# A hybrid decoder trunk: the order of TensorE's work written out by hand, projections in steps of 12 matmuls with mixer pieces between them

## The chip, the cores and the metric

The kernel runs on one core of a Trainium2 chip. The core has TensorE (PE, matmuls and transposes into PSUM), VectorE (DVE), ScalarE (ACT) and GpSimd (POOL) for elementwise work, and SyncE (SP), which issues the DMAs. Each engine runs its instructions in the order in which they stand in its queue and waits on semaphores for what the others produce. The metric is the device time of one execution in microseconds (us).

## The reference

The reference does one inference step of a 2-layer trunk of width 1024: 2048 prompt tokens from zero states, and 8 sample tokens from stored states. Cut to what matters:

```python
def hybrid_layer(x, ...):                     # called for layer 0 and 1, prompt and sample
    hn = rms_norm(x, norm_w)
    proj = hn @ w_in                          # 1024 -> 13 pieces, 256 wide; m_xbc is 512, m_dt 4
    r_q, r_k, r_v, r_g, g_q, g_f, g_i, g_g, s_u, s_g, m_z, m_xbc, m_dt = split(proj)
    o_ret  = head_rms(retention(rotary(r_q), rotary(r_k), r_v)) * silu(r_g)      # a, RetNet
    o_hgrn = head_rms(recurrence(silu(g_q), k(g_f), g_i, log_f(g_f))) * silu(g_g) # h, HGRN2
    gy     = gelu(s5_scan(s_u) + s5_D * s_u)                                      # s, S5
    o_s5   = gy * sigmoid(gy @ s5_glu_w + s5_glu_b) * silu(s_g)
    xbc    = silu(causal_conv(m_xbc))                                             # m, Mamba-2
    o_m2   = rms((ssd(xbc, softplus(m_dt)) + m2_D * xm) * silu(m_z)) * m2_norm_w
    return x + concat(o_ret, o_hgrn, o_s5, o_m2) @ w_out, final_states
```

A final RMSNorm follows. The outputs are both token streams and the six final states of each kind.

## The kernel before

The prompt goes through in 8 blocks: 2 layers of 4 blocks of `TB` = 512 tokens. The 8 sample tokens ("decode") ride along in the first block of each layer, that is in blocks 0 and 4. A block has nine phases: four input projections A, H, S and M, the mixers a, h, s and m that work on their results, and the output projection O. n and N are the norm of the next block.

A projection works in fp32 through TensorE's rounded format: each weight tile `wr` arrives by DMA, ACT casts it to a high part `wh` (L606, L642), DVE subtracts to get the low part (L607, L643), and PE does three matmuls (low times high, high times low, high times high) for each weight tile and token tile. `gemm` handles 256 columns (L590 with tokens on the output's partitions, L622 with columns on them), `gemm_wide` 512 columns (L647). Both hold their result in PSUM banks `gb` and read them out when all 8 slices of the contraction are done. The mixers, the norm and the decode step use banks `mb`. The two pools hold at most `NGP` = 5 and `NMP` = 3 banks.

The mixer h is a recurrence in seven levels. Each level has a small set of matmuls (L1183, the last level L1198) on a zero-padded copy of the queries that ACT writes (`zb`, L1176), then DVE merges the result under a mask (L1191) and scales queries and keys (L1204, L1205), from which ACT makes the next level's copy. m uses such a copy too, and the two buffers are handed out in turn (`zbuf`). s runs through matmuls L1284, a scan on DVE, matmuls L1332, transposes L1339 with a gelu on ACT (L1340), matmuls L1345 and a gate on DVE (L1348 to L1352), which writes the operand `mx` of O. a and m write theirs through transposes in `mix_store` (L663). L849 and L886 belong to the decode step.

What sets the order: the phases are emitted as the string `ORDER` says, one after the other, where `^` means the block before. This order gives the instructions their priorities. A list scheduler, at build time, then orders every engine's instructions, PE's too, by those priorities and its own model of when operands are there. The lines:

```python
ORDER = 'A-n^s-H-a-^OMh-SNm'
ORDER_LAST = 'A^sSa^OsHhMm'
```

So PE's queue is fixed when the kernel starts, and a mixer's few matmuls stand wherever the scheduler had them ready. WPRI, SPRI, DPRI and EPRI are offsets of priority for weight loads, the set-up of S5, decode, and the read-out of banks.

## Time and profile before

| | |
|---|---|
| median of 3 runs | 2356.22 us (2350.71 to 2357.18) |
| span of the profiled execution | 2351.3 us |
| time around it | 4.9 us to the median of the runs |
| PE busy | 2186.8 us, 93% |
| DVE busy | 1690.8 us, 72% |
| ACT busy | 1007.4 us, 43% |
| POOL busy | 247.0 us, 11% |
| mean granted TensorE clock | 0.973 |

An engine's busy time is the union of its instructions' spans. What is left to the span is idle, and a wait is put down to the instruction on another engine that ended last before it. A group of rows joins all instructions of one line, operation and operands; its mean is longer than its spacing, since matmuls overlap in the pipeline. In the timeline a row is a run of equal instructions: start, length, and in brackets the idle time before it with its releaser.

### The profile page before, as it was taken

To read this page: it belongs to the slowest core of one execution; us is meant where nothing else is said; L and a number is where in the kernel's file an instruction comes from. 1 tells how busy PE (TensorE), PEld (TensorE's weight loads), DVE (VectorE), ACT (ScalarE), POOL (GpSimd) and SP (SyncE) were. 2 spreads that over 40 slices of the span, in tenths; PEclk is the share of its full clock that TensorE was granted. 3 is DMA by queue.
4 is the path that set the end of the run, shared out by engine and by line. 5 is a ranking of instruction groups with operands and counts; after the bars stand their busy time and mean duration, and the time that the engine had idled before them with its cause. 6 is when DMAs were issued, how large, how long until landed. Compare 5 with 4: busy or idle time off the path is not lost.

```text
span 2351.3 us, 41033 instructions
## 1 busy us (share of the span) xinstructions
PE 2186.8 (93%) x15047; PEld 1724.8 (73%) x15047; DVE 1690.8 (72%) x4625; ACT 1007.4 (43%) x1873; POOL 247.0 (11%) x212
## 2 busy tenths in 40 slices
PE   7997899999989999999899987999999999999897
PEld 6766676686767877788676775776877787777687
DVE  6778885578866687558856588855985568766686
ACT  5334545245442353424534245443454344443543
POOL 1020011001111011001110001100011001100100
PEclk9998899999999999999999998999999999999998
DMA  5334543433434644251333424526244352337222
GB/s 190 89 95 103 159 154 76 129 107 118 133 101 147 139 126 141 75 167 47 125 126 114 134 65 153 162 46 182 86 153 157 104 175 64 95 122 260 64 65 83
DMA packets 259226, 283.89 MB, mean 121 GB/s; under 512 B 88208, under 2 KB 184608, under 8 KB 259024
## 3 DMA queue, kind: packets, MB, share of 16 engines
q1 hardware_dynamic: 259024, 281.26, 39.8%
q8 instruction: 119, 1.95, 0.3%
q14 instruction: 83, 0.68, 0.1%
HBM read 245.00 MB, written 31.99 MB: 118 GB/s over the span
## 4 chain that ended last, share of the span: by engine, by line
PE 57%; DVE 20%; issue 6%; ACT 3%; DMA 2%; SPq 1%; POOL 1%; ACTq 0%; DVEq 0%; POOLq 0%
PE gb L647 25%; PE gb L622 10%; PE gb L590 5%; DVE big L1191 2%; PE mb L1332 1%; PE mb L1183 1%; DVE wh L643 1%; PE mb L569 1%; DMA big<-s5c 1%; DVE hHb L1240 1%; DVE half L1299 1%; PE gb L652 1%; PE mb L663 1%; SPq L940 1%; PE mb L1198 1%
## 5 line engine op out<-in xcount | busy, mean ns | idle before, releaser
L647 PE MATMUL gb<-wh,hn 128*128 128x512 f32 x2208 | 558.0, 402 | 4.9 <-DVE wh L643 4.3
L622 PE MATMUL gb<-hn,wh 128*128 128x512 f32 x1920 | 491.5, 403 | 0.1
L647 PEld LDWEIGHTS gb<-wh,hn 128*128 128x128 f32 x2208 | 408.1, 190 | 110.3 <-issue 13.5
L622 PEld LDWEIGHTS gb<-hn,wh 128*128 128x128 f32 x1920 | 348.9, 188 | 89.4 <-issue 8.8
L642 ACT CAST wh<-wr 128x512 fp32r<-128x512 f32 x296 | 182.7, 620 | 375.9 <-PE gb L647 184.5
L647 PE MATMUL gb<-wh,mx 128*128 128x512 f32 x1344 | 338.0, 402 | 0.0
L643 DVE TENSOR_TENSOR wh<-wr,wh 128x512 fp32r<-128x512 f32 x296 | 208.6, 712 | 170.5 <-ACT wh L642 169.6
L607 DVE TENSOR_TENSOR wh<-wr,wh 128x512 fp32r<-128x512 f32 (+1 forms) x248 | 176.9, 724 | 169.5 <-ACT wh L606 163.6
L647 PEld LDWEIGHTS gb<-wh,mx 128*128 128x128 f32 x1344 | 247.7, 189 | 63.5 <-issue 6.9
L606 ACT CAST wh<-wr 128x512 fp32r<-128x512 f32 (+1 forms) x248 | 151.6, 621 | 268.1 <-PE gb L647 103.8
L590 PE MATMUL gb<-wh,hn 128*128 128x256 f32 (+1 forms) x1728 | 233.3, 291 | 4.2 <-DVE hn L553 4.1
L590 PEld LDWEIGHTS gb<-wh,hn 128*128 128x128 f32 x1728 | 218.2, 194 | 13.3 <-DVE hn L553 5.9
L1445 POOL TENSOR_TENSOR half<-mats,m_lal 128x512 fp32r<-128x512 f32 x64 | 71.7, 1148 | 511.1 <-DVE m_lal L1423 301.6
L1183 PE MATMUL mb<-zb,big 128*64 128x64 f32 x1536 | 66.5, 242 | 38.8 <-ACT zb L1176 31.5
L1191 DVE COPY_PREDICATED big<-lvl,mb 64x256 f32<-64x256 int32 x192 | 93.0, 537 | 10.3 <-PE mb L1183 6.4
L1176 ACT COPY zb<-big 64x512 f32<-64x512 f32 x112 | 70.3, 628 | 64.0 <-DVE big L1204 54.2
L1183 PEld LDWEIGHTS mb<-zb,big 128*64 128x64 f32 x1536 | 56.6, 152 | 53.5 <-ACT zb L1176 38.2
L1166 POOL TENSOR_TENSOR big<-mats,h_dg 128x1024 f32<-128x1024 f32 x16 | 34.0, 2140 | 557.8 <-DVE h_dg L1163 438.5
L1367 DVE SCALAR_TENSOR_TENSOR big<-gb,vt,big 128x511 f32<-128x511 f32 (+2 forms) x96 | 66.9, 739 | 12.0 <-ACT big L1365 11.8
L671 ACT ACTIVATE half<-mb 128x512 f32<-128x512 f32 x32 | 19.1, 598 | 88.3 <-PE mb L1227 47.8
L1348 DVE TENSOR_TENSOR half<-half,big 128x512 f32<-128x512 f32 x16 | 10.9, 687 | 63.1 <-ACT half L1347 63.1
L1042 POOL TENSOR_TENSOR half<-half,half 128x256 f32<-128x256 f32 x32 | 27.2, 850 | 235.0 <-DVE half L1040 85.2
(493 smaller groups left out, 3240.7 us busy)
## 6 DMA issues: line engine op xcount, KB each, us to landing
wr<-in_w_in SPq DMA_DIRECT2D x416, 256.0 KB
wr<-in_w_out SPq DMA_DIRECT2D x128, 256.0 KB
big<-s5c SPq DMA_DIRECT2D x56, 512.0 KB
xn<-xmid SPq DMA_DIRECT2D x32, 512.0 KB
xn<-in_x_prompt SPq DMA_DIRECT2D x24, 512.0 KB
xmid<-half SPq DMA_DIRECT2D x44, 256.0 KB
half<-xmid SPq DMA_DIRECT2D x44, 256.0 KB
half<-in_x_prompt SPq DMA_DIRECT2D x32, 256.0 KB
```

Of the source, the lines that this page charges most:

```text
L590: T.matmul(out, lhs[2 * ks[ki] + k][:, a, tt * P : (tt + 1) * P], hls[ki][:, c, k, :n], start=(ki == 0 and k == 0 and pi == 0 and tt % per ...
L606: S.copy(hl[:, 0, :, :n], raw[:, :, :n])
L607: V.tensor_tensor(hl[:, 1, :, :n], raw[:, :, :n], hl[:, 0, :, :n].bitcast(F32), ALU.subtract)
L622: T.matmul(banks[i], hl[:, a, k, i * P : (i + 1) * P], lhs[2 * k2 + k][:, c, :], start=(ki == 0 and k == 0 and pi == 0), stop=(ki == 3 and ...
L642: S.copy(hl[:, 0, 0:512], raw[:, 0:512])
L643: V.tensor_tensor(hl[:, 1, 0:512], raw[:, 0:512], hl[:, 0, 0:512].bitcast(F32), ALU.subtract)
L647: T.matmul(banks[tt], lhs[kt][:, a, tt * P : (tt + 1) * P], hl[:, c, 0:512], start=(kt == 0 and pi == 0), stop=(kt == KT - 1 and pi == 2))
L1176: S.copy(qz[sl, r, :].rearrange("p (b h) -> p b h", h=h), q[sl].rearrange("p a (b two h) -> p (a b) two h", two=2, h=h)[:, :, 1, :])
L1183: T.matmul(ps[su, j * 64 : (j + 1) * 64], k[:, j // 4, (j % 4) * P + 64 * u : (j % 4) * P + 64 * u + 64], qz[:, :, j * 64 + 32 * u : j * 6 ...
L1191: V.copy_predicated(stv[p][su, :, nu * u : nu * u + nu, :], mv, ps[su, p * 256 : p * 256 + 256].rearrange("p (c b h) -> p c b h", c=8, h=h))
L1367: V.scalar_tensor_tensor(acc[:, 3 - i :], ps[:, : TB - 3 + i], w(i), acc[:, 3 - i :], ALU.mult, ALU.add)
L1445: E('m').tensor_tensor(mm.rearrange("p (h t) -> p h t", h=4), tri[:, None, :].to_broadcast([P, 4, P]), lal[:, i, tt, :][:, :, None].to_bro ...
```

## The change

PE leaves the scheduler: `tc.manual_schedule` with PE alone keeps PE's instructions in the order in which the program emits them. DVE, ACT, POOL and SP are still ordered by the scheduler. To emit PE's work in a useful order, projections and mixers become generators. A projection yields after each step of 12 matmuls of 512 columns (or 24 of 256 or 260). `run` calls `tick` after each step, and `tick` lets at most two ready mixer streams (lanes m, s, a, h) and one of decode, layer load and set-up (lanes d, e, f, p) emit one piece each. `yield n` in a mixer says how many ticks to wait until its next piece. The core of the diff:

```diff
-ORDER = 'A-n^s-H-a-^OMh-SNm'
-ORDER_LAST = 'A^sSa^OsHhMm'
-EPRI = 0
+EPRI = 100
-DW = 2
-NWR = 7
-NWH = 6
+DW = 4
+NWR = 6
+NWH = 5
-NBIG = 9
+NBIG = 10
-NGP = 5
-NMP = 3
+NGP = 4
+NMP = 4
...
-    zbs = [ctile([P, 2, TB], f"zb{i}") for i in range(NZ)]
+    zbH, zbM = ctile([P, 2, TB], "zbH"), ctile([P, 2, TB], "zbM")
...
     def gemm_wide(lhs, w, c0, evac, dec=None):
...
+        for kt in range(KT - 2):
+            load(kt)
+            for tt in range(4):
+                t_pass(kt, tt)
+            dec_pass(kt)
+            yield
+        load(KT - 2)
+        load(KT - 1)
         for tt in range(4):
+            t_pass(KT - 2, tt)
+            t_pass(KT - 1, tt)
             with tc.high_priority(offset=EPRI):
                 evac(tt, banks[tt])
+            if tt == 1:
+                yield
...
     def mix_H(L, B):
...
+            yield 2
+            pss = []
             if l < 6:
                 ps = mbank()
...
+    def tick():
+        clock[0] += 1
+        for names, most in (("msah", 2), ("defp", 1)):
+            for st in front(names)[:most]:
+                st.step()
+
+    def drain(*streams):
+        for _ in range(10000):
+            left = [st for st in streams if st is not None and not st.done]
+            if not left:
+                return
...
+            min(heads, key=lambda st: st.ready).step()
+
+    def run(gen, each=None):
+        for n, _ in enumerate(gen):
+            if each is not None:
+                each(n)
+            tick()
...
+    with tc.manual_schedule(engines={mybir.EngineType.PE}):
...
+        for i, B in enumerate(blocks):
+            run(ga if i == 0 else gemm_A(B.L, B))
+            run(gemm_H(B.L, B))
+            if B.prev is not None:
+                finish(B.prev, ("a", B), ("h", B), parts=(0, 1) if nxt is not None else (0,))
...
+                run(gemm_M(B.L, B))
+                begin("m", B)
...
+                run(gemm_S(B.L, B), lambda n: next(norm, 0) if n >= 3 else None)
...
+                begin("s", B)
...
+            else:
+                run(gemm_S(B.L, B))
+                begin("s", B)
+                run(gemm_M(B.L, B))
+                begin("m", B)
+                finish(B.prev, parts=(1,))
+                finish(B)
```

`finish` runs O of the block given, here with a and h of the next block as streams beside it; `front` gives the streams whose waiting time is over, and `begin` starts a stream. The last two slices of `gemm_wide` are done bank by bank, so each bank is read out while the next is still filled; `gemm` does the same in its last step. Further edits: the decode step's bank comes from the `mb` pool, RV stands before RQ in A except in the first block, a is split into scores, state, inter and mixed pieces that overlap over token tiles, s loads its tables in halves, and s waits for h (`B.hdone`). In the last block, whose O has no later projections to stand beside, `drain` emits what is left of a, h, s and m in one go.

The instructions are the same on PE (11825 matmuls and transposes), DVE and POOL. ACT has 92 table loads in the program where it had 72, and there are 40 more DMAs (1290, 1250 before). In PE's order the projections' matmuls stand in 532 uninterrupted runs before and in 307 after; those 512 wide in 442 and in 265, and of the 442, 251 were shorter than 6 matmuls, of the 265 none.

On PE, the recurrence of h in the third block (`zb` is the padded copy, `hn` the projections' operand):

```order
L590 MATMUL gb_8632<-wh_8692,hn_5910 128x256 x5
L1183 MATMUL mb_8318<-zb_114,big_6968 64x64 x16
L590 MATMUL gb_8632<-wh_8692,hn_5910 128x256
L590 MATMUL gb_8633<-wh_8692,hn_5910 128x256 x6
L590 MATMUL gb_8632<-wh_8721,hn_5923 128x256 x2
L1183 MATMUL mb_8348<-zb_113,big_6968 64x64 x8
L590 MATMUL gb_8632<-wh_8721,hn_5923 128x256 x4
L590 MATMUL gb_8633<-wh_8721,hn_5923 128x256
L1183 MATMUL mb_8348<-zb_113,big_6968 64x64 x8
```

And now, where the levels of h (L1293) stand beside the output projection (L687) of the block before, with a's pieces (L1173 to L1202) and the decay sums (L1163):

```order
L1293 MATMUL mb_10209<-zbH,big_9640 64x64 x16
L687 MATMUL gb_10029<-wh_10239,mx_9932 128x512 x3
L687 MATMUL gb_10030<-wh_10239,mx_9932 128x512 x3
...
L687 MATMUL gb_10030<-wh_10256,mx_9425 128x512 x3
L687 MATMUL gb_10030<-wh_10261,mx_9531 128x512 x3
L1173 MATMUL mb_10287<-half_10207 128x128
...
L1211 MATMUL mb_10112<-big_9038,half_10174 64x64 x8
L1186 MATMUL mb_10326<-big_9038,half_9620 64x64 x4
L1202 MATMUL mb_10335<-hAb_111,half_10207 128x128 x2
L1163 MATMUL mb_10338<-mats,half_9635 128x128 x4
L1293 MATMUL mb_10345<-zbH,big_9640 64x64 x16
```

Between two levels there stood 9 matmuls of 256 columns, and the next level was cut in two; now eight rows of three matmuls of 512 columns and the pieces of a stand there.

On PE, the end of the last block, where s finishes (L1458 is what was L1332, L1466 L1339, L1474 L1345, and L620 is O's matmul, before L590):

```order
L1458 MATMUL mb_23160<-big_23154,big_22485 64x128 x2
L1466 MATMUL mb_23181<-mats,big_22714 128x128 x4
L1466 MATMUL mb_23187<-mats,big_22714 128x128 x4
L1474 MATMUL mb_23193<-big_23180,half_23178 128x512 x2
L1474 MATMUL mb_23203<-big_23180,half_23178 128x512 x2
L1765 MATMUL mb_23213<-mats,s_carry_22697 16x128
L620 MATMUL gb_23011<-wh_23219,mx_23200 128x256 x3
```

Before, projections of other blocks stood between these steps; here s goes from one to the next with nothing of the projections between.

## Rows read from the trace of the kernel before

**Rows 1.** The page: busy time of each engine, and the granted clock in 40 slices.

```profile
PE 2186.8 (93%) x15047; PEld 1724.8 (73%) x15047; DVE 1690.8 (72%) x4625; ACT 1007.4 (43%) x1873; POOL 247.0 (11%) x212
...
PEclk9998899999999999999999998999999999999998
```

**Rows 2.** The core's span and its mean granted clock.

```profile
core 0: 2351.3 us, clock 0.973
```

**Rows 3.** The page's costliest groups: busy us, mean ns, idle before and its releaser.

```profile
L647 PE MATMUL gb<-wh,hn 128*128 128x512 f32 x2208 | 558.0, 402 | 4.9 <-DVE wh L643 4.3
L622 PE MATMUL gb<-hn,wh 128*128 128x512 f32 x1920 | 491.5, 403 | 0.1
...
L647 PE MATMUL gb<-wh,mx 128*128 128x512 f32 x1344 | 338.0, 402 | 0.0
...
L590 PE MATMUL gb<-wh,hn 128*128 128x256 f32 (+1 forms) x1728 | 233.3, 291 | 4.2 <-DVE hn L553 4.1
...
L1183 PE MATMUL mb<-zb,big 128*64 128x64 f32 x1536 | 66.5, 242 | 38.8 <-ACT zb L1176 31.5
```

**Rows 4.** Waits of PE: total us, times, longest us.

```profile
PE mb L1183 <- ACT zb L1176: 31.5, 16, 5.4
PE mb L849 <- DVE half L847: 22.4, 6, 8.7
PE mb L1332 <- ACT big L1316: 13.8, 7, 3.1
...
PE mb L534 <- DMA mats<-in_c_mats: 6.6, 1, 6.6
```

**Rows 5.** The chain that ended last: start us, length us, what.

```profile
1004.42 33.34 PE gb L647 x144
...
1060.07 11.55 PE gb L590 x96
```

**Rows 6.** Timeline of PE, runs and their successors: start us, length us.

```profile
630.06 2.96 PE L622 MATMUL gb<-hn,wh 128*128 128x512 f32 x12
632.86 1.09 PE L1273 MATMUL mb<-mats,big 128*128 128x128 f32 x8
...
1456.76 0.94 PE L647 MATMUL gb<-wh,hn 128*128 128x512 f32 x3
1457.54 0.39 PE L1447 MATMUL mb<-half,strict_r 128*128 128x512 f32 x1
```

**Rows 7.** Two stretches, line L1183 alone: length, PE, PEld, clock, DMA share, GB/s.

```profile
219.00:240.00 21.00, 8.17 (x128) 7.24 (x128) 0.51 0.70 90
...
1071.00:1112.00 41.00, 7.35 (x192) 6.24 (x192) 1.00 0.12 36
```

**Rows 8.** Two stretches: length, PE, PEld, DVE, ACT, POOL, clock, DMA, GB/s.

```profile
450.00:500.00 50.00, 50.00 (x227) 37.44 (x226) 28.79 (x62) 16.23 (x26) 0.00 (x0) 1.00 0.58 172
...
1071.00:1112.00 41.00, 37.06 (x452) 31.45 (x450) 37.12 (x100) 20.39 (x35) 4.14 (x2) 1.00 0.12 36
```

**Rows 9.** Timeline of PE and DVE, the last s and the last m.

```profile
2177.90 5.53 PE L1332 MATMUL mb<-big,big 128*64 128x128 f32 x64 [3.12 <-ACT big L1316]
...
2188.52 3.70 PE L1345 MATMUL mb<-big,half 128*128 128x512 f32 x8 [0.45 <-ACT big L1340]
...
2193.95 0.67 DVE L1352 TENSOR_TENSOR mx<-half,mx 128x512 fp32r<-128x512 f32 x1
...
2306.56 0.44 PE L1468 MATMUL mb<-half,half 128*64 128x128 f32 x4
...
2312.15 0.70 PE L663 MATMUL mb<-mats,half 128*128 128x128 f32 x4 [1.18 <-DVE half L1491]
...
2314.31 25.89 PE L590 MATMUL gb<-wh,mx 128*128 128x256 f32 x204 [1.46 <-DVE mx L666]
```

**Rows 10.** Timeline of ACT around one table load.

```profile
1448.83 1.28 ACT L1428 ACT_TABLE_LOAD   x1
1450.13 0.21 ACT L1428 ACTIVATE m_ec<-mb 128x48 f32<-128x48 f32 x1
```

More of the change, by code (lines that the diff above doesn't have):

```diff
@@ L1 @@
+import copy
 import math
@@ L609, in gemm, with out @@
             raws.append(raw)
-            if mode == "T" and not late:
-                t_pass(ki, range(4))
-            elif mode == "T" and ki == 3:
-                for tt in range(4):
-                    for i in range(4):
-                        t_pass(i, (tt,))
-                for i in (1, 3):
-                    dec_pass(i)
-            elif mode == "F":
+        def out(i):
+            with tc.high_priority(offset=EPRI):
+                evac(i, banks[i][:, 0 : per * 256].rearrange("p (t c) -> p t c", t=2) if per == 2 else banks[i])
@@ new lines, in dec_pass @@
+        def dec_pass(ki):
+            for j in range(4 if dec is not None else 0):
+                T.matmul(dbank[32 * j : 32 * j + 8, :n], dec[0]()[:, 2 * ks[ki - 1 + j // 2] + j % 2, :], raws[ki - 1 + j // 2][:, j % 2, :n],
+                         start=(ki == 1), stop=(ki == 3))
+        if late:
+            for ki in range(4):
+                load(ki)
+            for tt in range(4):
+                for ki in range(4):
+                    t_pass(ki, tt)
+                if tt % per == per - 1:
+                    out(tt // per)
+                if tt == 3:
+                    for ki in (1, 3):
+                        dec_pass(ki)
+                    if dec is not None:
+                        dec[1](n, dbank)
+                yield
+            return
@@ L619, in gemm @@
+        for ki in range(4):
+            load(ki)
+            if mode == "T":
+                for tt in range(4):
+                    t_pass(ki, tt)
+                    if ki == 3 and tt % per == per - 1:
+                        out(tt // per)
+            elif ki < 3:
                 for k in range(2):
                     for i in range(2):
-                        for pi, (a, c) in enumerate(((1, 0), (0, 1), (0, 0))):
-                            T.matmul(banks[i], hl[:, a, k, i * P : (i + 1) * P], lhs[2 * k2 + k][:, c, :],
-                                     start=(ki == 0 and k == 0 and pi == 0), stop=(ki == 3 and k == 1 and pi == 2))
@@ L624, in gemm @@
-            if ki % 2 == 1 and not late:
-                dec_pass(ki)
-        for i in range(nb):
-            with tc.high_priority(offset=EPRI):
-                evac(i, banks[i][:, 0 : per * 256].rearrange("p (t c) -> p t c", t=2) if per == 2 else banks[i])
-        if dec is not None:
-            dec[1](n, dbank)
+                        f_pass(ki, k, i)
+            else:
+                for i in range(2):
+                    for k in range(2):
+                        f_pass(ki, k, i)
+                    out(i)
@@ L1492, in mix_M, with out_proj @@
             ogs.append(og)
-        mix_store(B.mix, 6, lambda tt: ogs[tt], L.m2_w)
-    def out_proj(L, B, src, dst, last):
+        masks(0)
+        for tt in range(5):
+            yield 2
+            if tt > 0:
+                second(tt - 1)
+            if tt < 4:
+                first(tt)
+            if tt < 3:
+                masks(tt + 1)
+        yield 4
+        yield from mix_store(B, 6, lambda tt: ogs[tt], L.m2_w)
+        if B.last:
+            save_ssm(B.l)
+    def out_proj(L, B, src, dst, last, parts=(0, 1)):
         w = A["w_out"][L.l]
@@ L1600, in zeroed, with __init__, can, step @@
         return t
[L1602 removed]
     nblk = DEPTH * NB
[L1604 to L1606 removed]
+    clock = [0]
+    class Stream:
+        def __init__(self, gen, pri, alt_, most):
+            self.gen, self.pri, self.alt, self.most = gen, pri, alt_, most
+            self.ready, self.cond, self.done = clock[0], None, False
+        def can(self):
+            return self.cond is None or self.cond()
+        def step(self):
+            alt[0] = self.alt
+            with tc.high_priority(offset=self.pri):
+                y = next(self.gen, "end")
+            alt[0] = ""
+            self.cond, self.ready = None, clock[0]
+            if y == "end":
+                self.done = True
+            elif callable(y):
+                self.cond = y
+            else:
+                self.ready += min(y or 0, self.most)
@@ new lines, in trunk_kernel, with spawn, front @@
+    lanes = {"m": [], "s": [], "a": [], "h": [], "d": [], "e": [], "f": [], "p": []}
+    def spawn(lane, gen, pri=0, alt_="", most=9):
+        st = Stream(gen, pri, alt_, most)
+        lanes[lane].append(st)
+        return st
+    def front(names):
+        out = []
+        for n in names:
+            while lanes[n] and lanes[n][0].done:
+                lanes[n].pop(0)
+            if lanes[n] and lanes[n][0].can() and lanes[n][0].ready <= clock[0]:
+                out.append(lanes[n][0])
+        return sorted(out, key=lambda st: st.ready)
@@ new lines, in mixer, with begin, begin_dec, mix_all @@
+        yield from {"a": mix_A, "h": mix_H, "s": mix_S, "m": mix_M}[ph](B.L, B)
+    def begin(ph, B):
+        B.st[ph] = spawn(ph, mixer(ph, B), most=1 if B.prev is None and ph in "ah" else 9)
+    def begin_dec(B, which):
+        for ph in which:
+            d = copy.copy(B.dec)
+            f = {"a": d.mix_A, "h": d.mix_H, "s": d.mix_S, "m": d.mix_M}[ph]
+            B.st["d" + ph] = spawn("d" if ph in "am" else "e", f(), DPRI, "d")
+        if "s" not in which:
+            return
+        def mix_all():
+            yield lambda: all(B.st["d" + ph].done for ph in "ahms")
+            yield from B.dec.mix_all()
+        B.st["dO"] = spawn("f", mix_all(), DPRI, "d")
```

623 lines of the change are left out of this document (350 added, 273 removed).

## The prediction

> **What bounds the kernel now.** I read the page first: PE is busy 2186.8 of 2351.3 us, 93%, DVE 72%, ACT 43% [rows 1, 2]. So PE sets the end, and a gain must come from its 164.5 idle us (2351.3 − 2186.8) or from a shorter busy time. The groups of PE come next, with the mean spacing that they imply. The three groups of 512-wide projection matmuls hold 558.0 + 491.5 + 338.0 = 1387.5 us for 5472 matmuls, 0.2536 us each [rows 3]. In an unbroken run at full clock the chain shows 33.34/144 = 0.2315 us, and 11.55/96 = 0.120 us for 256 columns [rows 5]. So 5472 × 0.2315 = 1267 us would do, and 120 us are excess.
>
> The timeline shows one source: where another piece cuts in, the next matmul comes later. A run of 12 takes 2.80 us to its successor, 0.233 each; a run of 3 takes 0.78 us, 0.26 each [rows 6]. Per run this is 0.02 to 0.09 us in these two places, and I take 0.13 as the mean of a cut, an estimate that lies above both, because the load of other weights behind a run falls on the next group's rows as well. Before, 442 runs of 512-wide matmuls are cut: 442 × 0.13 = 57 us.
>
> The other source is the clock. The mean granted clock is 0.973 [rows 2]. If all that is missing is time at 1.2 rather than 2.4 GHz, it is 0.027 × 2351.3 / 0.5 = 127 us. One such stretch, 219 to 240 us, has clock 0.51, and line L1183 takes 8.17/128 = 0.064 us per matmul there, against 7.35/192 = 0.038 between 1071 and 1112 us at clock 1.00 [rows 7]. The clock's digit falls to 8 in only four of the 40 slices, so the low stretches are short and scattered [rows 1]. I give the clock the rest of the excess, 120 − 57 = 63 us.
>
> Last, the waits: PE waits 16 times for the padded copy of the recurrence, 31.5 us; six times in the decode step, 22.4 us; seven times for s, 13.8 us; once for its first operand, 6.6 us [rows 4]. The wait of one kind is thus 2.0 to 3.7 us where it comes. They come where pieces of mixers stand too close: between two levels of the recurrence there is at least ACT's copy and DVE's merge, and only 9 short projection matmuls stood there in the block that the change's listing shows (9 × 0.120 = 1.1 us). Where projections run alone, PE has no gap at all and DVE is 58% busy (28.79 of 50 us); where mixers crowd, DVE is 91% busy (37.12 of 41 us) and PE waits [rows 8]. The work is uneven, not too much.
>
> **The change part by part.** All of it is one sum against the span, 2351.3 us.
>
> *Idle time.* Today there are 164.5/532 = 0.31 us per run of projections. Afterwards 307 runs are left, and 24 matmuls of 512 columns, 24 × 0.24 = 5.8 us, stand between two levels. The mean wait of 2.0 us for the copy, on top of the 1.1 us of projections that stood there, fits into that. I keep 0.31 us for each place: 307 × 0.31 = 95 us, so −69. It includes what cannot go: 6.6 us until PE's first operand [rows 4] and the end after PE's last matmul, 2314.31 + 25.89 = 2340.2 to 2351.3, or 11.1 us [rows 9]. Bounds: down to 0.1 us for each place, if pieces are always ready (31 us and those 18 at the ends, 49 in all, −115); up to 0.9 us, if one place in four waits as the decode step did (3.7/4), 276 us, +112. I take 0.31, nearest to the rows of today's mean, because the new places are further apart, yet all of them hold up PE when late.
>
> *512-wide matmuls.* 265 cuts are left, 265 × 0.13 = 34 us. With fewer stretches of mixers alone I let half of the clock's 63 us go, 32 stay. 1267 + 34 + 32 = 1333, so −54. Bounds: 0, and −86 if the whole clock part goes.
>
> *256- and 260-wide.* Line L590 on `hn` has 233.3 us for 1728, against 1728 × 0.120 = 208, an excess of 25; with the same 45% that the excess above loses, −11.
>
> *Mixers.* PE's other work is short matmuls. L1183 takes 66.5/1536 = 0.043 us in the mean and 0.038 at full clock [rows 3, 7]: 1536 × 0.005 = 8 us in this line alone. For all mixer lines I take −15, about double, and bounds 0 and −40.
>
> *The end of the last block.* Here s and m are emitted without projections between. In the trace of before, s goes from the end of L1332 (2177.90 + 5.53 = 2183.4) to its last operand of O at 2194.6, 11.2 us, of which its own matmuls are 4.7 [rows 9]: 6.5 are exposed. m goes from the end of L1468 at 2307.0 to the first L590 at 2314.3, of which 0.7 is L663; 6.6 us, and 1.18 + 1.46 are waited for already: 4.0 more [rows 9]. Together +10.
>
> *Added loads.* Twenty table loads more at 1.28 us are 26 us on ACT, 1007 + 26 = 1033 us of some 2212, 47%. The load is followed by the next activation within 0.02 us [rows 10]. ACT's slack hides them: 0. If one stood in a chain that PE waits for, it is 1.3 us, and all twenty 26, the upper bound. Forty more DMAs lie beside a DMA share of 0.58 in projections [rows 8]: 0. Seven to six raw weight buffers, six to five split ones: 0, since a step of 12 matmuls (2.9 us) uses up one of the five split buffers, so the split can run four steps, 11.6 us, ahead; if it is late, PE waits at the start of a step, and that is inside the bound of 0.9 us for each place.
>
> Sum: 2351.3 − 69 − 54 − 11 − 15 + 10 = 2212 us. The median of the runs shown is 4.9 us above the span, so 2217 us.
>
> **The rivals.**
>
> *Nearly no waits.* If every piece is ready, the idle part is 49 us in place of 95, and the time 2217 − 46 = 2171 us. For it: where projections run alone, PE has no gap [rows 8]. Against it: a, h, decode and s all use the same DVE queue, whose order the scheduler still makes from its own model. Chance 0.16.
>
> *DVE becomes the bound.* DVE's 1690.8 us stay. My forecast asks for 1690.8/2212 = 76% in the mean over the whole program, head and end too. If dependences keep it at 0.73 to 0.74, the span cannot be below 1690.8/0.735 = 2300 us, the time 2305. For it: 0.72 is all it reached so far [rows 1], and read-out of banks is now four deep. Against it: 91% over 41 us [rows 8] shows that it can be fed better. Chance 0.17.
>
> *The clock does not rise.* The many short waits that stay might keep the clock down as the long ones do. Then the clock's share of the terms is not saved: 31 in the 512-wide matmuls, some 5 in the others, 15 in the mixers, 51 in all: 2268 us. The stretch at 1071 us speaks against it: PE idles 41 − 37.06 = 3.9 us in it, in pieces, at 1.00 [rows 8]. Chance 0.07. The Trainium skill has the rule for this rival ("TensorE: Matmul & The Clock Gate", section "A second HAM failure mode: psum-queue depth-cycling"): brief idling between groups of matmuls, as banks are cycled, is enough to send the clock back and forth. The trace does not agree in that stretch; by the page this rival would be the likeliest one.
>
> *Slower: a rigid PE.* A list scheduler puts a mixer's piece where its model has it ready. A count of ticks does not know of readiness, and one late piece holds up the projection behind it, which delays reading out banks, which are now 4 for projections, all of them in use in one `gemm_wide`. Without idle time the sum above is 2212 − 95 = 2117 us, so the change loses from (2351.3 − 2117)/307 = 0.76 us for each place. At 0.9 (one place in four waits 3.7 us, as L849 [rows 4]) it is 2117 + 276 = 2393, or 2398 us. Against it: PE's queue was as rigid before, since the order was made at build time. Chance 0.10.
>
> *Nothing changes.* The waits go from one place to another, at 0.72 of DVE as now: within 0.3% (7 us, about what a measurement of this kernel can tell from no change) of 2356. Chance 0.04.
>
> **How the numbers follow.** The forecast, 2217 us, has 0.46, with a range of its own of 2185 to 2260. Faster by over 0.3%: 0.46 + 0.16 + 0.07 and 0.16 of the 0.17 for DVE, 0.85. Within 0.3%: 0.04 + 0.01 = 0.05. Slower: 0.10. For 8 in 10 the range goes from 2150, below the case without waits, to 2320, above most of the DVE case; outside are the rigid PE, no change, and the tails of the other cases, about 0.19.
>
> **What would show it.** PE's busy time should fall to 2212 − 95 = 2117 us and its share rise to 96%; if busy time falls as said and idle time does not, the steps on matmuls are right and the one on waits is wrong. The 512-wide groups should stand at 0.244 us each (1333/5472). The mean clock should be 0.985 or more. The recurrence's wait for the padded copy, 31.5 us, should be under 10. At the end of the last block two gaps of about 6 us each should show before O's matmuls. DVE should be 76% busy. The forecast is wrong if PE waits over 0.76 us for each place, if the clock stays at 0.973, or if DVE is above 90% over whole blocks with PE waiting for it.

## The result, and the profile after

The changed kernel takes 2296.84 us (median of 4 runs, 2295.91 to 2297.80) against 2355.83 us before: 59 us or 2.4% less, a ratio of 0.9758 with a 95% interval of 0.9744 to 0.9772. The forecast was 2217 us. The direction was right; the gain is 59 us where the sum said 139. The time lies inside the wide range of 2150 to 2320 us, but above the 2185 to 2260 of the forecast's own mechanism.

The page of the changed kernel, parts 1 and 2, to be held against [rows 1]:

```profile
PE 2140.4 (93%) x15047; PEld 1732.4 (76%) x15047; DVE 1668.9 (73%) x4625; ACT 1037.3 (45%) x1893; POOL 236.4 (10%) x212
...
PEclk9998899999999999999999999999999999999988
```

Its core, to be held against [rows 2]:

```profile
core 0: 2294.3 us, clock 0.965
```

PE's busy time fell by 46.4 us. Its idle time, 2294.3 − 2140.4 = 153.9 us, fell by only 10.6, and the mean clock is lower than before, not higher. The groups of the projections, to be held against [rows 3] (L687 is what was L647, L625 L622, L620 L590, L1293 L1183):

```profile
L687 PE MATMUL gb<-wh,hn 128*128 128x512 f32 x2208 | 542.0, 401 | 3.7 <-DVE half L1626 3.6
L625 PE MATMUL gb<-hn,wh 128*128 128x512 f32 x1920 | 489.0, 408 | 7.0 <-DVE half L1118 7.0
...
L687 PE MATMUL gb<-wh,mx 128*128 128x512 f32 x1344 | 339.3, 405 | 7.4 <-DVE half L1700 6.9
...
L620 PE MATMUL gb<-wh,hn 128*128 128x256 f32 (+1 forms) x1728 | 225.2, 291 | 2.1 <-DVE hn L556 1.1
...
L1293 PE MATMUL mb<-zbH,big 128*64 128x64 f32 x1536 | 58.2, 232 | 5.2 <-ACT half L1165 3.5
```

The 512-wide matmuls take 1370.3 us, 0.2504 each; 1333 was forecast. The recurrence's line lost 8.3 us of busy time and 33.6 of its 38.8 us of waits. But other waits stand in their place. By releaser, PE's listed waits are 57.0 us for ACT, 85.1 for DVE and 8.4 for DMA before, and 11.6, 102.8 and 27.2 after: what ACT held up is gone, and DVE and DMA hold up more. Waits of PE (total us, times, longest), to be held against [rows 4]:

```profile
PE mb L1458 <- DMA big<-s5c: 14.2, 14, 4.0
PE mb L722 <- DVE half L736: 13.2, 3, 4.9
PE mb L1328 <- DVE big L1307: 10.5, 4, 5.9
PE mb L1608 <- DVE half L1597: 8.4, 1, 8.4
PE gb L625 <- DVE half L1118: 7.0, 4, 5.1
PE gb L687 <- DVE half L1700: 6.9, 10, 1.1
PE mb L534 <- DMA mats<-in_c_mats: 6.5, 1, 6.5
```

Where in the program was the time gained? I gave each matmul its spacing at full clock (0.2315 us for 512 columns, 0.12 for 256, 0.075 for 128, 0.04 for 64), summed these along PE's timeline, and cut both traces where a quarter and nine tenths of the sum are done. The prices of the short matmuls are rounded, so the cuts are estimates. The three stretches of the kernel before, and then of the changed one (length, PE, PEld, DVE, ACT, POOL, clock, DMA share, GB/s):

```profile
0.00:624.70 624.70, 564.14 (x3832) 435.86 (x3833) 464.69 (x1374) 267.13 (x506) 74.05 (x75) 0.96 0.41 120
624.70:2112.30 1487.60, 1406.58 (x9613) 1107.30 (x9611) 1054.90 (x2795) 641.65 (x1164) 150.93 (x124) 0.98 0.40 122
2112.30:2351.30 239.00, 216.13 (x1606) 181.67 (x1605) 171.25 (x458) 98.60 (x203) 22.02 (x13) 0.97 0.37 116
```

```profile
0.00:607.20 607.20, 545.27 (x3796) 435.77 (x3797) 464.60 (x1424) 276.41 (x520) 64.87 (x67) 0.95 0.43 123
607.20:2039.80 1432.60, 1379.65 (x9529) 1110.93 (x9528) 1035.63 (x2720) 663.09 (x1177) 154.16 (x133) 0.98 0.43 128
2039.80:2294.30 254.50, 215.46 (x1725) 185.68 (x1724) 168.64 (x482) 97.82 (x197) 17.32 (x12) 0.92 0.35 109
```

| stretch of the work | length | PE idle before | PE idle after |
|---|---|---|---|
| first quarter | −17.5 us | 60.6 us | 61.9 us |
| middle, 0.25 to 0.9 | −55.0 us | 81.0 us | 53.0 us |
| last tenth | +15.5 us | 22.9 us | 39.0 us |

The idle columns do not hang on where exactly the cuts fall, the lengths do: cut by the projections' matmuls alone, the three differences are about −6, −84 and +33 us. So the middle gains, 28 us of it in waits; the first quarter waits as before; the last tenth gives some of the gain back, with 16 us more of idle time, at a clock of 0.92.

### The profile page after: what moved, and what is told of

Same layout as the page of the kernel before. It is cut to its first block, busy times and chain, and to the rows that moved or that the text cites. A ratio compares the mean times of both kernels' runs of the same rounds, so it can differ in the third digit from the quotient of the medians.

```text
span 2294.3 us, 41082 instructions
## 1 busy us (share of the span) xinstructions
PE 2140.4 (93%) x15047; PEld 1732.4 (76%) x15047; DVE 1668.9 (73%) x4625; ACT 1037.3 (45%) x1893; POOL 236.4 (10%) x212
## 5 line engine op out<-in xcount | busy, mean ns | idle before, releaser
L687 PE MATMUL gb<-wh,hn 128*128 128x512 f32 x2208 | 542.0, 401 | 3.7 <-DVE half L1626 3.6
L625 PE MATMUL gb<-hn,wh 128*128 128x512 f32 x1920 | 489.0, 408 | 7.0 <-DVE half L1118 7.0
L687 PEld LDWEIGHTS gb<-wh,hn 128*128 128x128 f32 x2208 | 411.3, 189 | 109.8 <-issue 13.8
L625 PEld LDWEIGHTS gb<-hn,wh 128*128 128x128 f32 x1920 | 361.7, 193 | 98.0 <-issue 11.9
L681 DVE TENSOR_TENSOR wh<-wr,wh 128x512 fp32r<-128x512 f32 x296 | 216.3, 735 | 273.2 <-ACT wh L680 271.7
L687 PE MATMUL gb<-wh,mx 128*128 128x512 f32 x1344 | 339.3, 405 | 7.4 <-DVE half L1700 6.9
L687 PEld LDWEIGHTS gb<-wh,mx 128*128 128x128 f32 x1344 | 250.0, 191 | 75.6 <-DVE half L1700 11.6
L620 PE MATMUL gb<-wh,hn 128*128 128x256 f32 (+1 forms) x1728 | 225.2, 291 | 2.1 <-DVE hn L556 1.1
L620 PEld LDWEIGHTS gb<-wh,hn 128*128 128x128 f32 x1728 | 217.6, 196 | 5.6 <-issue 2.6
L1284 ACT COPY zbH<-big 64x512 f32<-64x512 f32 x112 | 70.8, 632 | 46.7 <-PE mb L1293 39.4
L1293 PE MATMUL mb<-zbH,big 128*64 128x64 f32 x1536 | 58.2, 232 | 5.2 <-ACT half L1165 3.5
L1293 PEld LDWEIGHTS mb<-zbH,big 128*64 128x64 f32 x1536 | 51.9, 145 | 14.5 <-issue 7.7
L1458 PE MATMUL mb<-big,big 128*64 128x128 f32 x512 | 40.7, 304 | 18.2 <-DMA big<-s5c 14.2
L620 PE MATMUL gb<-wh,mx 128*128 128x256 f32 x384 | 51.1, 298 | 4.6 <-DVE mx L1481 4.1
L620 PEld LDWEIGHTS gb<-wh,mx 128*128 128x128 f32 x384 | 50.0, 204 | 6.1 <-DVE mx L1481 4.9
```

The costliest lines, as they stand in the source:

```text
L620: T.matmul(o, lhs[2 * ks[ki] + k][:, a, tt * P : (tt + 1) * P], hls[ki][:, c, k, :n], start=(ki == 0 and k == 0 and pi == 0 and tt % per = ...
L625: T.matmul(banks[i], hls[ki][:, a, k, i * P : (i + 1) * P], lhs[2 * ks[ki] + k][:, c, :], start=(ki == 0 and k == 0 and pi == 0), stop=(ki ...
L681: V.tensor_tensor(hl[:, 1, 0:512], raw[:, 0:512], hl[:, 0, 0:512].bitcast(F32), ALU.subtract)
L687: T.matmul(banks[tt], lhs[kt][:, a, tt * P : (tt + 1) * P], hls[kt][:, c, 0:512], start=(kt == 0 and pi == 0), stop=(kt == KT - 1 and pi = ...
L1284: S.copy(qz[sl, r, :].rearrange("p (b h) -> p b h", h=h), q[sl].rearrange("p a (b two h) -> p (a b) two h", two=2, h=h)[:, :, 1, :])
L1293: T.matmul(ps[su, j * 64 : (j + 1) * 64], k[:, j // 4, (j % 4) * P + 64 * u : (j % 4) * P + 64 * u + 64], qz[:, :, j * 64 + 32 * u : j * 6 ...
```

## The experiments

Every kernel below is the changed one with one edit, except where it says otherwise. The median of the changed kernel, 2296.84 us, is the mark, and the ratios are to the kernel before, which ran beside each. In six kernels (the changed one, e8, e10, e12, e17 and e18) PE's instructions stand in the same order, form by form; what differs is the work and the order of the other engines.

### Is it the last block? (e1, e5, e4, e17)

e1 moved the projection M and the mixer m of the last block ahead of H and S:

```diff
             run(ga if i == 0 else gemm_A(B.L, B))
+            if nxt is None:
+                run(gemm_M(B.L, B))
+                begin("m", B)
             run(gemm_H(B.L, B))
```

> The changed kernel with one edit: in the last block the projection M and with it the mixer m stand right after A, before H, S and O, so that m's serial pieces lie beside projections and not beside the last O. Theory (the gain of the middle of the program is given back in the last block, where PE waits for m and s, 26 us in brackets between 2150 and 2250 us): the waits for DVE's products of m (8.4 and 4.1 and 4.8 us) go, the clock of the last 100 us rises above 0.9, and the time falls by 15 to 30 us, to 2267 to 2282. Rival (the end is not special, the waits are spread evenly): within 5 us of 2297. Rival (DVE's queue is full anyway, m only displaces h): 2297 to 2310.

2306.92 us (0.9804, 0.9780 to 0.9829), 10 us slower than the mark. m's waits went and others came: 4.6 and 8.8 us in front of L722, 12.3 us in front of L1458. e5 gave the last block 23 us more of projection beside its mixers:

```diff
-            if B.prev is not None:
-                finish(B.prev, ("a", B), ("h", B), parts=(0, 1) if nxt is not None else (0,))
+            if B.prev is not None and nxt is not None:
+                finish(B.prev, ("a", B), ("h", B))
...
-                finish(B.prev, parts=(1,))   # behind A, H, S and M; now A, H, M and S
+                finish(B.prev)
```

> The changed kernel with one edit: in the last block the whole output projection of the block before stands behind A, H, M and S, instead of its first half between H and S and its second behind M. So h and a run beside M and S, and m and s have 46 us of that projection beside them before the last O, not 23. Theory (what the end loses is cover: mixers emitted with nothing beside them; moving m ahead only passed the wait on to a and s): the waits after 2150 us fall from 26 to under 10 us and the time by 15 to 30 us, to 2267 to 2282. Rival (it is DVE's queue, full of the read-out of the last outputs, or the final chain s, O that no order hides): within 5 us of 2297 or above.

2300.29 us (0.9779, 0.9745 to 0.9812): no gain. m's two waits ahead of L1608, 12.5 us, are gone, and 9.2 us for a transfer stand in front of L1458. So more cover alone does not shorten the end. e4 filled the waits of the end with matmuls of no use:

```diff
         def step(self):
+            if tail[0]:
+                filler(10)                   # 10 matmuls 128x512 into a spare bank
             alt[0] = self.alt
```

> The changed kernel with ten extra 512-wide matmuls of no use, into a bank of the mixers' pool, ahead of each mixer piece that is emitted while the last block's O runs (about 2.3 us each at full clock). They do nothing for the result. Theory that the low clock behind waits is a cost of its own (the 48 and 173 matmuls of O after the waits took 7.65 and 23.6 us where 5.8 and 20.8 are full speed): the clock of the last 100 us rises, O's runs fall to 0.120 us per matmul, and the time stays or falls by 3 to 8 us although PE has 20 us more to do. Rival (the clock is only a mark of the waits, and work in front of a late piece delays it): 2300 to 2320 us.

2301.36 us (0.9778, 0.9763 to 0.9793). The stretch from 2170 to 2290 us, of the changed kernel and then of e4:

```profile
2170.00:2290.00 120.00, 86.24 (x633) 75.82 (x631) 71.49 (x196) 40.79 (x94) 11.52 (x8) 0.85 0.31 100
```

```profile
2170.00:2290.00 120.00, 106.65 (x752) 92.75 (x750) 67.94 (x173) 38.67 (x88) 10.09 (x8) 0.96 0.29 90
```

PE does 20 us more here and the clock rises from 0.85 to 0.96, while the run is 4.5 us longer. The low clock thus goes with the waits, and most of the added work fits into them, so at the end it is not PE's work that bounds. The clock rose as the theory said, the time is the rival's. What the higher clock gave back is not separated from what the filler delayed. e17 left PE's order and changed what DVE takes first at the end (with the shared buffers of e8):

```diff
-            with tc.high_priority(offset=EPRI):
+            with tc.high_priority(offset=epri[0]):   # -200 in the last block's O of the block before
                 evac(tt, banks[tt])
```

> The changed kernel with the shared padded buffers of e8 and, in the last block alone, the output projections' read-out of banks at a priority offset of -200 in place of 100, so that DVE takes m's products ahead of the last outputs' sums and norms. Theory (at the end m waits for DVE's order, not for DVE's load or for cover): the waits for L1597 and for L1700 in front of m, 12.5 us at the end, fall below 4, and the time is 2268 to 2282, 5 to 19 us under e8. Rival (m's own chain takes that long, or the late read-out holds up O): 2284 to 2300 us.

2294.46 us (0.9753, 0.9731 to 0.9775), 7 us over e8, with intervals that just touch. DVE took m's product ahead of the final norm, 2.7 us of which stand in front of it in the changed kernel. The wait of 8.3 us in m became 5.4, the one of 4.2 us stayed at 4.0, and 4.1 us came up in front of s. The theory of this run fell too.

### Is it decode, or the first block? (e2, e3, e6, e7)

e2 and e3 leave the decode tokens out, e2 of the changed kernel and e3 of the one before. The edit of e3:

```diff
-    blocks[0].dec = Dec(L, A["x_sample"].rearrange("b o d -> b (o d)"))
...
-                if B.last:
-                    nb_.dec = Dec(layers[nb_.l], blocks[(nb_.l - 1) * NB].dec.dst)
```

> The changed kernel without the 8 decode tokens: their norm, projections, mixers, states and outputs are left out in both layers. It is to be compared with the same cut of the kernel before. Theory (the first two blocks gained nothing because DVE is full there, 95% busy from 150 to 300 us, with decode and set-up): without decode the difference between before and after grows from 59 us to 75 to 95 us. Rival (decode hides as well or as badly in either, the loss is elsewhere): the difference stays at 50 to 65 us. Either way the time falls, by 60 to 110 us, since DVE and PE have less to do.

> The kernel before without the 8 decode tokens (their norm, projections, mixers, states and outputs are left out). Theory: it falls less than the changed kernel does, by 40 to 80 us, to some 2275 to 2315 us, so that the changed kernel without decode is 75 to 95 us ahead. Rival: both fall by the same amount within 6 us.

2186.77 us after the change, 2215.20 before it: the difference shrinks from 59 to 28 us where the theory said it would grow. Decode costs 137.6 us in the kernel before (2352.77 beside it) and 110.1 in the changed one. So decode does not spoil the gain; about half of the gain is that decode now fits in better. The waits for L847, 22.4 us [rows 4], are gone; the rest was not followed. The pages of e2 and e3:

```profile
PE 2055.9 (94%) x14435; PEld 1698.8 (78%) x14435; DVE 1534.4 (70%) x4231; ACT 996.8 (46%) x1809; POOL 237.9 (11%) x212
```

```profile
PE 2091.2 (94%) x14435; PEld 1696.6 (77%) x14435; DVE 1569.0 (71%) x4231; ACT 969.9 (44%) x1789; POOL 248.2 (11%) x212
```

In spans of 2181.5 and 2213.8 us, PE is idle for 125.6 and 122.6 us. Without decode the change thus saves no idle time at all; its whole gain there is busy time. e6 started decode's a and h earlier, e7 the first block's a:

```diff
+            if B.dec:
+                begin_dec(B, "ah")           # e6, behind H; only "m" is left behind M
...
+            if B.prev is None:
+                begin("a", B)                # e7, beside H
             run(gemm_H(B.L, B))
```

> The changed kernel with one edit: the decode mixers a and h start right behind the block's projection H, not behind M, in the first block of each layer. DVE is 52% busy from 100 to 150 us and 97% from 150 to 200 us. Theory (the first block is late because DVE's work is bunched): the waits between 150 and 300 us, 29 us, fall by 5 to 15 us, the time by 5 to 20 us. Rival (decode pieces hold up the prompt's mixers whenever they come): 2295 to 2310 us.

> The changed kernel with one edit: in the first block the mixer a starts behind A, beside H, not together with h behind H. Theory (bunched work in the first block): the waits at 156 to 200 us (3.9, 2.6, 4.1 us) go and the time falls by 5 to 15 us. Rival: the wait moves on to h or the norm and the time stays within 3 us.

2308.64 us (0.9816, 0.9800 to 0.9832) and 2301.08 us (0.9782, 0.9763 to 0.9801). In both the waits moved on: e6 has 8.7, 7.6 and 8.6 us between 160 and 230 us at other lines, e7 6.0 and 3.7 us for the padded copy. Both theories fell. e6's rival held; of e7's, the wait moved on as it said, but the time is 4 us above the mark, not within 3.

### Does the order by hand gain, or the other edits? (e9, e18, e12, e8)

e9 gives PE back to the scheduler and keeps all else:

```diff
-    with tc.manual_schedule(engines={mybir.EngineType.PE}):
+    with ExitStack():
```

> The changed kernel with PE left to the scheduler again, as in the kernel before: the steps, streams and pieces are emitted in the same order, but that order is only the priority; all other edits stay. Theory (the order by hand is what gains: the middle's gain of 55 us comes from steps of 12 that are not cut): 2330 to 2380 us, with over 400 runs of projections on PE. Rival (the new order of emission, banks read out one by one and the other edits gain, whoever orders PE): 2280 to 2310 us.

2697.34 us (1.1453, 1.1420 to 1.1486), far beyond either theory. Its page, and PE's timeline in a stretch of it:

```profile
PE 2550.6 (95%) x15047; PEld 1851.9 (69%) x15047; DVE 1682.0 (62%) x4625; ACT 1040.5 (39%) x1893; POOL 247.7 (9%) x212
```

```profile
706.71 0.43 PE L1458 MATMUL mb<-big,big 128*64 128x128 f32 x2
707.07 0.49 PE L625 MATMUL gb<-hn,wh 128*128 128x512 f32 x1
707.50 0.43 PE L1458 MATMUL mb<-big,big 128*64 128x128 f32 x2
707.86 0.50 PE L625 MATMUL gb<-hn,wh 128*128 128x512 f32 x1
```

PE is no more idle than in the changed kernel (148 against 153.9 us), but busy for 410 us longer. The scheduler spread the pieces out one matmul at a time: one of the projection and two of s take 0.79 us (706.71 to 707.50), of which the projection alone would need 0.23 and the two of s, by an unbroken run of 32 in the changed kernel (1.90 us), 0.12. Counted in PE's timeline, projections stand in 1612 runs here, 469 before and 278 in the changed kernel (decode's matmuls are no cut here, as they were in the 532 and 307 above). The busy time differs by 410 us over 1334 runs, 0.31 us per run, where the forecast took 0.13; some of it is the lower clock, 0.961 against 0.965.

e9 shows that the new order of emission needs PE's order by hand. It does not price that order against the one before, which the scheduler made from the old emission. All six kernels with one PE order are faster than the kernel before beside them, by 26 (e18) to 66 us (e8), but they share the other edits too; the buffer counts and s's halved tables were not undone.

e18 undid the read-out bank by bank, with PE's order unchanged:

```diff
             t_pass(KT - 1, tt)
-            with tc.high_priority(offset=EPRI):
-                evac(tt, banks[tt])
             if tt == 1:
                 yield
+        for tt in range(4):
+            with tc.high_priority(offset=EPRI):
+                evac(tt, banks[tt])
```

> The changed kernel with the four banks of a 512-wide projection read out in one go behind its last matmul, as before the change, in place of one by one while the next bank is filled; PE's order is unchanged. Theory (with four banks for projections, all in use, the next projection's first matmul waits for the read-out): waits in front of projection matmuls, now 22 us, rise by 10 to 30 us and the time by 10 to 40 us. Rival (DVE takes them in the same order anyway): within 5 us of 2297.

2327.97 us (0.9890, 0.9872 to 0.9909), 31 us slower, as the theory said. Its waits in front of the next projection rose from 6.9 to 16.5 us, and PE was busy for 21 us more, at a clock of 0.957:

```profile
PE gb L687 <- DVE half L1701: 16.5, 6, 5.5
```

e12 took back the priority of the read-out:

```diff
-EPRI = 100
+EPRI = 0
```

> The changed kernel with the offset of priority for reading out banks at 0, as before, not 100. Theory (the read-out of banks ahead of the mixers' products on DVE makes m and a late, as L1608 behind L1700): the waits for L1597 and L736 fall, 2280 to 2297 us. Rival (late read-out holds up the next projection): 2297 to 2330 us, with waits in front of projection matmuls (L687, L625, L620), now 22 us, above 40.

2318.78 us (0.9860, 0.9845 to 0.9874), 22 us slower, the rival's time; the waits in front of projections came to 35 us, not above 40. The waits for s's tables grew from 14.2 to 24.9 us, and one of 10.6 us for the padded copy came up. e8 took back the two separate padded buffers:

```diff
-            qz = zbH
+            qz = zbuf()                      # m likewise, two buffers in turn
```

> The changed kernel with the two zero-padded buffers handed out in turn again, as before, in place of one for h and one for m. Theory (the gain of the middle comes from PE's order, 24 matmuls between two levels): within 4 us of 2297, and no wait for the padded copy comes back beyond 3 us. Rival (the split of the buffers is what removed the 31.5 us of waits for the padded copy): 2305 to 2330 us.

2286.99 us (0.9716, 0.9699 to 0.9734): 10 us faster than the changed kernel, and the fastest of all; neither theory nor rival had that. One wait for the padded copy is left:

```profile
PE mb L1304 <- ACT zb L1288: 2.0, 1, 2.0
```

So it is not the split of the buffers that removed the 31.5 us. In e9, where the scheduler orders PE, the waits for this copy are 2.6 us in all: the new order of emission, or another of the shared edits, removes them, whoever orders PE. One place where e8 gained is told below.

### Is it DVE's load, or the distances? (e10, e11, e13 to e16)

e10 and e11 put half of the 512-wide subtractions on GpSimd, in the changed kernel and in the one before:

```diff
-                V.tensor_tensor(hl[:, 1, 0:512], ...)
+                (G if kt % 2 else V).tensor_tensor(hl[:, 1, 0:512], ...)
```

> The changed kernel with the subtraction for the low part of every second 512-wide weight tile on GpSimd, 148 instructions of 0.73 us less on DVE (108 us). Theory (what is left of PE's waits is DVE's lateness, since DVE is 95% busy where PE waits): PE's idle time falls by 15 to 40 us and the time by 15 to 45 us, to 2252 to 2282. Rival (the waits are latencies of chains, which a less busy DVE does not shorten, or GpSimd slows DVE while it works): 2290 to 2320 us.

> The kernel before with the same subtractions on GpSimd. Theory: PE waited for DVE there too, but a scheduler that puts another matmul in front hid more of it; it gains 0 to 20 us, less than the changed kernel gains. Rival: it gains as much as or more than the changed kernel.

2305.60 us (0.9811, 0.9784 to 0.9837), in the rival's range, and 2407.05 us (1.0232, 1.0214 to 1.0249), a loss of some 55 us that neither theory nor rival of e11 had. Page of e10, its new group on GpSimd, and PE's waits:

```profile
PE 2134.6 (93%) x15047; PEld 1724.7 (75%) x15047; DVE 1629.6 (71%) x4477; ACT 1037.3 (45%) x1893; POOL 438.3 (19%) x360
```

```profile
L681 POOL TENSOR_TENSOR wh<-wr,wh 128x512 fp32r<-128x512 f32 x148 | 201.4, 1361 | 987.1 <-ACT wh L680 808.3 <-issue 73.5 <-DMA wr<-in_w_out 29.0
```

```profile
PE mb L722 <- DVE half L736: 14.8, 3, 5.9
...
PE mb L1328 <- DVE big L1307: 10.0, 4, 5.9
PE mb L1608 <- DVE half L1597: 8.2, 1, 8.2
```

The line itself gave DVE 105 us back, its busy time fell by 39, and the long waits are much the same: 13.2, 10.5 and 8.4 us became 14.8, 10.0 and 8.2. So 39 us less on DVE do not shorten them. It is a weak test of DVE's load, though: the same move costs the kernel before 55 us, so it has a price of its own, and DVE is still 71% busy. e13 to e16 moved the distances in ticks:

```diff
-        yield 3                              # ahead of h's last part
+        yield 5                              # e13 and e14; e15: 6; e16: 1
...
-        yield 3                              # ahead of a's store
+        yield 5                              # e13, e14; e16: 1
```

> The changed kernel with longer distances ahead of the pieces that wait: 5 ticks, not 3, ahead of a's store and of h's last part (L1328), 5 for 4 ahead of m's store, 4 for 3 ahead of h's store. Theory (what PE still waits for are latencies of single chains, set too close by the counts of ticks; with 108 us less on DVE they stayed the same): the waits for L736, L1637 and L1307, 28.5 us in the changed kernel, fall below 10 and the time by 10 to 25 us, to 2272 to 2287. Rival (a piece that comes later makes the next one late, and the end longer): 2295 to 2315 us.

> As e13, and 3 ticks for 2 ahead of s's second matmuls and its gate, and the padded buffers shared in turn as before the change. Theory: the waits for s's tables and gate weights (19 us) fall by half as well, and with the 10 us that the shared buffers gave: 2258 to 2278 us. Rival: 2285 us or more.

> The changed kernel with one number changed: 6 ticks, not 3, ahead of h's last part (L1328), which waits 5.9 us in the seventh block and 3.1 in the sixth. Theory (a latency of one chain): the 10.5 us of waits for L1307 go, and with the clock that falls behind them the time falls by 8 to 16 us, to 2281 to 2289. Rival (waits move on): 2294 to 2300.

> The reverse: 1 tick, not 3, ahead of a's store, h's last part and h's store, and 2 for 4 ahead of m's store. Theory (single chains): each of some 32 pieces comes 6 us earlier than now, so waits of up to 3 to 6 us each come up: 2330 to 2400 us. Rival (distance does not matter since something else releases them): within 8 us of 2297.

Longer: 2313.47 us (0.9830, 0.9812 to 0.9849), with e14's further edits 2301.98 (0.9786, 0.9763 to 0.9808), h alone 2305.85 (0.9803, 0.9783 to 0.9822). Shorter: 2357.75 us (1.0016, 1.0000 to 1.0031), the whole gain lost. The theory of e16 held, those of e13, e14 and e15 fell. The waits of e13, and of e16:

```profile
PE mb L1338 <- DVE hHb L1357: 18.0, 10, 7.3
PE mb L1608 <- DVE half L1595: 11.1, 1, 11.1
PE mb L722 <- DVE half L736: 9.0, 2, 4.9
```

```profile
PE mb L722 <- DVE half L736: 29.3, 10, 7.0
PE mb L1338 <- DVE hHb L1357: 16.8, 9, 3.5
PE mb L722 <- DVE half L1637: 14.2, 5, 4.8
```

Distances matter, and the changed kernel's are the best of those tried: shorter ones bring the waits in front of a's and m's stores up by 26 us, longer ones take h's wait for L1307 away and bring 18.0 us, for 1.6 before, to h's next pieces.

### What the waits are

One of the longest, in the changed kernel: L1328 waits 5.9 us at 1862 us for one product of h. PE's rows:

```profile
1856.47 0.27 PE L1328 MATMUL mb<-mats,big 128*128 128x128 f32 x1
1862.65 1.75 PE L1328 MATMUL mb<-mats,big 128*128 128x128 f32 x7 [5.91 <-DVE big L1307]
1864.33 5.14 PE L625 MATMUL gb<-hn,wh 128*128 128x512 f32 x12
1869.30 0.60 PE L1338 MATMUL mb<-hHb,big 128*128 128x128 f32 x4
```

DVE's queue meanwhile:

```profile
1852.85 0.42 DVE L1306 TENSOR_TENSOR big<-big,h_t 128x256 f32<-128x256 f32 x1
1853.19 2.74 DVE L1721 SCALAR_TENSOR_TENSOR half<-half,fn_rs,half 128x512 f32<-128x512 f32 x4
1855.84 0.69 DVE L608 TENSOR_TENSOR wh<-wr,wh 128x512 fp32r<-128x512 f32 x1
1856.56 0.75 DVE L1499 SCALAR_TENSOR_TENSOR big<-gb,vt,big 128x511 f32<-128x511 f32 x1
...
1861.97 0.22 DVE L1502 SCALAR_TENSOR_TENSOR big<-convc,vt,big 128x3 f32<-128x3 f32 x1
...
1862.18 0.42 DVE L1307 TENSOR_TENSOR big<-big,h_t 128x256 f32<-128x256 f32 x1
```

L1307 takes 0.42 us and follows on L1306, which was done at 1853.3. It stands 9 us further back in the queue, behind the final norm of finished outputs, a weight tile and the convolution's read-out. Nothing in it is slow, and DVE itself waited for nothing: it ran without a gap for these 9 us, in the order that the scheduler had made. In e8 the same products of h stand ahead of that norm and that read-out:

```profile
1855.83 0.42 DVE L1311 TENSOR_TENSOR big<-big,h_t 128x256 f32<-128x256 f32 x1
...
1856.31 0.42 DVE L1311 TENSOR_TENSOR big<-big,h_t 128x256 f32<-128x256 f32 x1
...
1857.50 2.74 DVE L1725 SCALAR_TENSOR_TENSOR half<-half,fn_rs,half 128x512 f32<-128x512 f32 x4
```

There PE does not wait. The wait also shows its price: the 12 matmuls behind it take 4.97 us (1864.33 to 1869.30), where a run of 12 takes 2.80 [rows 6]. The granted clock is 0.54 from 1864.3 to 1869.3 us.

## Why the prediction fell short

In the span 82 of the forecast 139 us are missing: 48 of idle time (the +10 at the end counted in it) and 34 of busy time.

*Idle time, −69.* This is the step that failed: measured, −10.6. It took the mean wait per run of projections, 0.31 us, as a property of a cut. It is not: with 278 runs in place of 469 the idle time is 153.9 in place of 164.5 us, and e9 has 1612 runs and 148 us. Waits sit at a few places, and their number does not go with the cuts. What the runs put in its place: PE's queue is made by hand, DVE's still by the scheduler, and of PE's listed waits 102.8 us, 18 more than before, are for DVE. At the place above PE waits because a short product stands late in DVE's queue. The six kernels with one PE order support this: they lie between 2287.0 and 2328.0 us by what the other engines do. It is not shown for every wait: those for s's tables, 14 us, are transfers, and an experiment with DVE's order by hand was not made.

*512-wide matmuls, −54.* Measured −17, the second step that was off. In the changed kernel's timeline a run of 12 at full clock takes 2.86 us to its successor, 0.238 each, no less than before the change:

```profile
2121.34 3.01 PE L625 MATMUL gb<-hn,wh 128*128 128x512 f32 x12
2124.20 0.60 PE L1338 MATMUL mb<-hHb,big 128*128 128x128 f32 x4
```

The clock's part did not halve: 0.035 × 2294.3 / 0.5 = 161 us are at the lower clock where 127 were. The clock stayed low where waits are, 0.92 in the last tenth and 0.54 behind the wait at 1862 us. So the condition of the rival "the clock does not rise" came true, and the 31 us that the sum had counted on here were not saved; that the short waits do it, as the rival said, is not shown, for long waits stayed as well. The Trainium skill's rule that was weighed there ("TensorE: Matmul & The Clock Gate", section "A second HAM failure mode: psum-queue depth-cycling"), by which brief idling between groups of matmuls sends the clock back and forth, would have given the better forecast of the clock's direction. No run here separates brief idling from long waits.

*The size of a cut.* 0.13 us was an estimate above both rows that it was taken from, and too low for e9, which gives 0.31. That a cut also costs the group behind it is seen there: two matmuls of s take 0.36 us (706.71 to 707.07), not 0.12. With 0.31, 191 runs less are worth 59 us, and 34 us more at the lower clock cost some 17: −42, beside the −46 measured for busy time. The two errors, too little for a cut and too much for the clock, hid each other in part; that last sum is argued, not shown, since e9's cuts are of single matmuls.

*256- and 260-wide, −11, and mixers, −15.* Measured −8 for line L620 on `hn`; for all other PE work 46.4 − 17.2 − 8.1 = 21 us less, 8.3 of them in the recurrence's line, where 8 were forecast. Both were right in kind.

*End of the last block, +10.* The last tenth has 16 us more of idle time. The wait in s was as forecast, 2.2 us ahead of L1474 and 4.1 ahead of L620, and m's last one is 4.8 us ahead of L722. Two waits of m before that, 4.1 us ahead of L1608 for the sum of a last output (L1700) and 8.4 us for a product of m (L1597) that stands behind the final norm in DVE's queue, were not in the sum.

*Read-out bank by bank.* The forecast gave it no price of its own. Undone it costs 31 us (e18), half of the gain, so without it the sum would have been further off.

*Added loads, 0.* 92 table loads stand in the program, and ACT is 45% busy; no wait of PE names one. The added transfers were put at 0 as well. Those for s's tables, now in halves, became PE's largest wait, 14.2 us; the corresponding line L1332 waited 13.8 us for ACT [rows 4], so here a wait changed its releaser.

*The rivals.* "DVE becomes the bound" has the nearest number, 2305 us, and its sign: DVE stays at 73%. Its mechanism, that dependences keep DVE there and so set the end, is neither shown nor ruled out: 39 us less on DVE brought nothing (e10), and with the same DVE work e8 is 10 us faster. "A rigid PE" as a loss did not come; its mechanism, a late piece that holds up what stands behind it, is seen at the place above and likely took much of the missing gain, which is argued.

## What to carry to other kernels

What an order written by hand for one engine gains depends on the order of the engines that it waits for. Look in the timeline at what stands ahead of the awaited instruction in its queue before moving the waiting one. A mean wait per cut is no price for a cut: price waits by the places where they stand, with their chain, and take busy time per cut from a trace where cuts are many. Small edits that remake the other engines' order move this kernel by some 10 us either way (e8 down, e15 up) and by more (e12, 22 us up), so a gain of that size is no proof of the reason for it.

## What the runs showed of the hardware

- Alternating single projection matmuls with pairs of s's matmuls (128 columns on half of the array) costs 0.79 us per group at full clock, where the two parts in unbroken runs need 0.23 and 0.12 (e9); over the program about 0.31 us per run, the clock's part included.
- Behind a wait of 5.9 us the next 12 matmuls ran 2.1 us longer than the 2.86 us at full clock, at a granted clock of 0.54; filled with useless matmuls, a stretch rose from clock 0.85 to 0.96, and the run became 4.5 us longer (e4).
- GpSimd takes 201.4/148 = 1.36 us for the subtraction that DVE does in 0.73. Taking 105 us from one line of DVE lowered its busy time by only 39 us (e10); its other lines took longer, and the cause was not tried.
